# Shifted convolution copies through a DRAM scratch tile, and VectorE operands in the free halves of PSUM banks

## Chip, cores and metric

The kernel runs on one core of a Trainium2 chip, in one launch. The metric is the device time of one execution in microseconds (us). Three executions of the kernel before took 1400.87, 1400.93 and 1402.88 us; the median is 1400.93 us. A core has TensorE (PE in the profile, with its weight loads as PEld), VectorE (DVE), ScalarE (ACT), GpSimd (POOL) and SyncE (SP), which here issues every DMA.

## The reference, cut to what matters

One decoder layer over 256 tokens and 2048 channels in float32. Two head groups read the same projected input; the change touches both.

```python
h = rms_norm(x, norm_mix_pre); z = h @ w_cat
z_rwkv = z + (prev - z) * mu                    # token shift of the first 3360 columns
# RWKV-7 time mixing: 16 heads of 64
kk = heads(k * k_k); kk = kk / max(sqrt(sum(kk*kk)), 1e-12)
y = wkv7_scan(r, decay, k, v, -kk, kk * iclr)   # delta-rule state update, token by token
y = group_norm(y) * gn_gain + gn_bias
y = (y + bonus) * gate
# Conformer convolution: 1024 channels, causal, depthwise, width 31
u = u_lin * sigmoid(u_gate)
c = depthwise_conv(u, dw_w) + dw_b; c = silu(layer_norm(c))
x = x + rms_norm(concat(y, c) @ w_out, norm_mix_post)
# then a squared-ReLU MLP (2048 -> 8192 -> 2048) and a gated embedding of p
```

## The kernel before, in words

**Layout.** Channels lie on the 128 partitions and tokens in the free direction, so a tile is 128 channels by 256 tokens (`T`). Every weight matrix comes in units of 1 MB (16 blocks of 128x128, lines 312 and 384 to 399) into two buffers `W`. `split_stream` (line 401) turns each quarter of a unit into a rounded part `wh` (ACT, line 285) and a remainder `wl` (mostly POOL, line 248), with seven buffers of each. `tile_task` (line 418) multiplies a tile: in the first stage three matmuls of 256 columns for each of 16 blocks (lines 434 to 436), later two matmuls of 512 and 256 columns (lines 439 to 442).

**Order.** The instruction order of each engine is written by a small planner, `Plan` (line 98). Work is given as generators that take buffers (`Take`), wait for conditions (`Wait`) and yield operations with an estimated cost; `run` issues the operation that can start first by the estimates, and among those near it the one of the smallest priority number. The order so found is fixed in each engine's queue. DMAs all go in one queue, SP, in the planner's order (lines 210 to 213): an issue moves the planner's SP clock by 60 ns, and the landing is put 1,900 ns behind the transfer.

**First stage** (to about 555 us). `ORDER` (line 62) lists the input tiles: three for each of eight pairs of heads (`p`), two for each of eight blocks of convolution channels (`c`). All share two PSUM banks `acc`.
- `zshift` (line 619) evicts an input tile of a pair: DVE scales it into `zp` (SBUF, and the bank is free again), ACT makes `zt` = (1-mu) zp, and DVE adds mu times the shifted `zp` (line 252).
- `keys`, `chunk_mats`, `values`, `bonus`, `inverse` and `recur` (lines 692 to 971) do the time mixing of a pair. `recur` runs one pair after the other (`seqlock`) and accumulates in the bank `psy`; ACT copies `psy` to `ysb`, and `group_norm` (line 976) goes on from there, on DVE for most of it.
- `ev_lin` and `ev_gate` (lines 1011, 1021) make `u` = linear part times sigmoid of the gate. `taps` (line 1035) does the convolution as matmuls over four channels-by-shift copies: for each group of 32 channels, four matmuls with columns of the identity matrix put `u`, shifted by 0 to 3 tokens, onto four blocks of 32 partitions in a bank `wk` (line 1044), ACT copies the bank into `cvst` (line 1047, recorded as line 285), and 32 matmuls take the 31 taps from it (line 1056).
- `layer_norm` (line 1066) runs over all eight blocks when the last is done.
- The output projection follows, the convolution half first (`OUT_ORDER`, line 64). Its split input uses the buffer `hl` that the input tiles read, so it waits for the last of them.

**Second stage.** Normalisation, MLP, gate; nothing of it is changed.

Of the kernel before, what the change touches and what calls it, by code (L numbers as in the profile page):

```python
# [16 lines left out]
P = 128  # L17
T = 256
# [79 lines left out]
class Plan:  # L98
# [100 lines left out]
    def issue(self, task, best):  # L199
# [123 lines left out]
def decoder_block(ctx: ExitStack, tc: tile.TileContext, x, p, w_in, w_gd, w_out, w_up, w_down,  # L323
# [225 lines left out]
    pl.static("cv", cvst)  # L549
    def v4(t):  # L550
        return t.rearrange("p (c t) -> p c t", c=NC)
# [62 lines left out]
    def scaled(acc, o, W, cols=P):  # L614
        yield Wait(lambda: "rstd" in S)
        r = S["rstd"]
        yield pl.tt(["DVE"], o, acc.t[:cols, :T], r.t[:cols], ALU.mult, T, [acc, r], [W], [acc])

    def zshift(acc, o, W, mu, j=0, cols=P):
        zp = yield Take("zp", 1)  # L620
        yield pl.memset(zp.t[:, 0:1], 0.0, [(zp, 0)], 1)
        yield from scaled(acc, zp.t[:cols, 1:], zp, cols)
        mu, om = vec(mu, j, rows=cols), omu[:cols, VOFF[mu] + j if VOFF[mu] < 24 else 24 + VOFF[mu] - VOFF["mu_wa"] + j:][:, 0:1]
        d = yield Take("zt", 1)
        yield pl.act(d.t[:cols], zp.t[:cols, 1:], AF.Identity, T, [zp, "omu"], [d], scale=om)
        a, b = zp.t[:cols, 0:T], d.t[:cols]
# [65 lines left out]
    def keys(j):  # L692
# [12 lines left out]
        n4 = yield Take("n4")  # L705
        yield pl.ts(["DVE"], n4.t, psn.t[:, 0:4], 1e-24, None, ALU.max, None, 4, [psn], [n4], [psn])
# [3 lines left out]
        yield pl.act(n4.t, n4.t, AF.Sqrt, 4, [n4], [n4])  # L710
        yield pl.tt(PD, kp.t, kp.t, zk.t, ALU.mult, T, [kp, zk], [kp], [zk])
        rn = yield Take("rn")
        yield pl.vec(80, lambda: nc.vector.reciprocal(n4.t, n4.t), [n4], [n4])
        yield pl.vec(202, lambda: nc.vector.tensor_copy(rn.t, n4.t[:, :, None].to_broadcast([P, 4, C])),
                     [n4], [rn], [n4])
# [79 lines left out]
    def bonus(j):  # L795
# [4 lines left out]
        yield pl.stt(rk.t, zr.t, vec("r_k", j), kp.t, ALU.mult, ALU.mult, T, [zr, kp], [rk], [zr, kp])  # L800
        pb = yield Take("wk")
        yield pl.pe(430, lambda: nc.tensor.matmul(pb.t[:, :T], bones, rk.t, start=True, stop=True),
                    [rk], [pb], [rk])
        bv = yield Take("bv")
# [21 lines left out]
    def inverse(j):  # L826
# [10 lines left out]
        ud = yield Take("ud")  # L837
        yield pl.vec(335, lambda: nc.vector.tensor_reduce(out=ud.t, in_=um.t.rearrange("p c q j -> p c j q"),
                                                          axis=mybir.AxisListType.X, op=ALU.add), [um], [ud], [um])
        udh = yield Take("udh")  # L840
        udl = yield Take("udl")
        yield pl.copy(["DVE"], udh.t, ud.t, 32, [ud], [udh])
        yield pl.tt(["DVE"], udl.t, ud.t, udh.t.bitcast(F32), ALU.subtract, 32, [ud, udh], [udl], [ud])
# [6 lines left out]
        pe = yield Take("inv")  # L850
# [62 lines left out]
    def recur(j):  # L913
# [62 lines left out]
    def group_norm(j, ysb):  # L976
        pr = prs[j]
        X3 = mybir.AxisListType.X
        s4 = yield Take("s4")
        yield pl.vec(335, lambda: nc.vector.tensor_reduce(out=s4.t, in_=ysb.t, axis=X3, op=ALU.add), [ysb], [s4])  # L980
        yield pl.ts(["DVE"], s4.t, s4.t, 1.0 / 64, None, ALU.mult, None, 4, [s4], [s4])
        cen = yield Take("cen")
        yield pl.tt(["DVE"], cen.t, ysb.t, s4.t[:, :, None].to_broadcast([P, 4, C]), ALU.subtract, T,
                    [ysb, s4], [cen], [s4])
# [8 lines left out]
        pgn = yield Take("psy")  # L993
# [27 lines left out]
    def ev_gate(j):  # L1021
        def f(acc):
            gt = yield Take("gt")
            yield from scaled(acc, gt.t, gt)
            yield pl.act(gt.t, gt.t, AF.Sigmoid, T, [gt], [gt])
# [3 lines left out]
            yield pl.tt(PD, lin, lin, gt.t, ALU.mult, T, [gt, u], [u], [gt])  # L1029
# [5 lines left out]
    def taps(j):  # L1035
# [478 lines left out]
```

## Time and profile before

| | |
|---|---|
| median of three runs | 1400.93 us |
| profiled execution, its own time | 1402.03 us |
| its span | 1400.2 us |
| PE busy | 1351.5 us (97%) |
| POOL busy | 1174.2 us (84%) |
| ACT busy | 799.4 us (57%) |
| DVE busy | 736.4 us (53%) |
| DMA moved | 229.40 MB, 164 GB/s |

The profile is that of one execution. Busy time is the union of an engine's instructions. A PE instruction's recorded end is modelled and overlaps its successor, so what an instruction costs PE is read from its start to the next one's start. An idle stretch stands in front of an instruction with what ended it ("<-").

### The profile page before, as it was taken

To read this page: it belongs to the slowest core of one execution; us is meant where nothing else is said; L and a number is where in the kernel's file an instruction comes from. 1 tells how busy PE (TensorE), PEld (TensorE's weight loads), DVE (VectorE), ACT (ScalarE), POOL (GpSimd) and SP (SyncE) were. 2 spreads that over 40 slices of the span, in tenths; PEclk is the share of its full clock that TensorE was granted. 3 is DMA by queue.
4 is the path that set the end of the run, shared out by engine and by line. 5 is a ranking of instruction groups with operands and counts; after the bars stand their busy time and mean duration, and the time that the engine had idled before them with its cause. 6 is when DMAs were issued, how large, how long until landed. Compare 5 with 4: busy or idle time off the path is not lost.

```text
span 1400.2 us, 27458 instructions
## 1 busy us (share of the span) xinstructions
PE 1351.5 (97%) x10476; PEld 1182.8 (84%) x10476; DVE 736.4 (53%) x1305; ACT 799.4 (57%) x1667; POOL 1174.2 (84%) x1002
## 2 busy tenths in 40 slices
PE   8999999999789999999999999999999999999898
PEld 7868878788778998788888888888888888889688
DVE  7256837235886545687003663236632266433694
ACT  6835665556657656855445554455554455555853
POOL 7765756576777769789999999999999999999787
PEclk9999999999899999999999999999999999999999
DMA  7442333433222465345555554555554555555353
GB/s 243 159 140 95 115 130 113 137 110 137 91 99 95 153 248 182 128 160 194 211 182 191 194 185 181 183 189 194 187 181 182 187 194 189 181 181 190 124 198 120
DMA packets 40354, 229.40 MB, mean 164 GB/s; under 512 B 6304, under 2 KB 9632, under 8 KB 14624
## 3 DMA queue, kind: packets, MB, share of 16 engines
q1 hardware_dynamic: 40224, 227.66, 46.0%
q8 instruction: 82, 1.34, 0.4%
q14 instruction: 48, 0.39, 0.1%
HBM read 225.55 MB, written 2.10 MB: 163 GB/s over the span
## 4 chain that ended last, share of the span: by engine, by line
PE 86%; DVE 8%; ACT 2%; issue 1%; DMA 1%; POOL 1%; SPq 0%; DVEq 0%; ACTq 0%; POOLq 0%
PE acc L441 34%; PE acc L442 17%; PE acc L434 8%; PE acc L435 7%; PE acc L436 7%; PE acc L440 3%; PE inv L1056 2%; PE acc L439 1%; PE wk L1044 1%; DVE hl L252 1%; DVE acc L246 1%; DVE acc L252 1%; PE psy L930 1%; PE seq L938 1%; PE wk L749 1%
## 5 line engine op out<-in xcount | busy, mean ns | idle before, releaser
L248 POOL TENSOR_TENSOR wl<-W,wh 128x512 fp32r<-128x512 f32 x548 | 734.4, 1353 | 119.2 <-ACT wh L285 99.3
L285 ACT CAST wh<-W 128x512 fp32r<-128x512 f32 x568 | 346.3, 618 | 220.3 <-PE acc L440 69.0
L441 PE MATMUL acc<-hl,wh 128*128 128x512 f32 x1016 | 369.8, 403 | 11.3 <-DVE hl L252 5.7
L441 PE MATMUL acc<-fhl,wh 128*128 128x512 f32 x806 | 288.2, 395 | 0.0
L442 PE MATMUL acc<-hl,wl 128*128 128x256 f32 x1016 | 286.5, 282 | 0.0
L434 PE MATMUL acc<-hl,wh 128*128 128x256 f32 (+1 forms) x928 | 282.1, 304 | 1.0 <-DVE zp L246 0.9
L436 PE MATMUL acc<-hl,wl 128*128 128x256 f32 (+1 forms) x928 | 265.2, 286 | 6.3 <-POOL wl L248 6.0
L435 PE MATMUL acc<-hl,wh 128*128 128x256 f32 (+1 forms) x928 | 265.7, 286 | 3.2 <-DVE hl L252 2.0
L248 POOL TENSOR_TENSOR wl<-Wb,wh 128x512 fp32r<-128x512 f32 x173 | 237.0, 1380 | 18.4 <-ACT wh L285 11.2
L441 PEld LDWEIGHTS acc<-hl,wh 128*128 128x128 f32 x1016 | 192.1, 189 | 60.2 <-DVE hl L252 8.4
L442 PE MATMUL acc<-fhl,wl 128*128 128x256 f32 x806 | 227.2, 282 | 0.0
L442 PEld LDWEIGHTS acc<-hl,wl 128*128 128x128 f32 x1016 | 193.2, 190 | 3.7
L434 PEld LDWEIGHTS acc<-hl,wh 128*128 128x128 f32 (+1 forms) x928 | 179.2, 193 | 15.6 <-issue 10.1
L246 DVE TENSOR_TENSOR gt<-acc,tb 128x256 f32<-128x256 f32 x124 | 52.4, 423 | 263.7 <-ACT tb L276 263.1
L436 PEld LDWEIGHTS acc<-hl,wl 128*128 128x128 f32 (+1 forms) x928 | 179.1, 193 | 7.3 <-POOL wl L248 6.6
L435 PEld LDWEIGHTS acc<-hl,wh 128*128 128x128 f32 (+1 forms) x928 | 179.5, 193 | 5.4 <-DVE hl L252 3.7
L441 PEld LDWEIGHTS acc<-fhl,wh 128*128 128x128 f32 x806 | 151.5, 188 | 33.4
L285 ACT CAST wh<-Wb 128x512 fp32r<-128x512 f32 x174 | 107.6, 621 | 89.4 <-PE acc L440 35.5
L442 PEld LDWEIGHTS acc<-fhl,wl 128*128 128x128 f32 x806 | 151.3, 188 | 2.7
L246 DVE TENSOR_TENSOR f<-f 128x256 f32<-128x256 f32 x63 | 85.9, 1366 | 1.9
L246 DVE TENSOR_TENSOR fhl<-f,fhl 128x256 fp32r<-128x256 f32 x62 | 58.5, 946 | 26.0 <-ACT fhl L276 26.0
L248 POOL TENSOR_TENSOR wlb<-W,whb 128x512 fp32r<-128x512 f32 x50 | 69.2, 1384 | 1.9 <-ACT whb L285 1.6
(319 smaller groups left out, 2004.2 us busy)
## 6 DMA issues: line engine op xcount, KB each, us to landing
W<-in_w_up_dram SPq DMA_DIRECT2D x43, 1024.0 KB, 4.8
W<-in_w_down_dram SPq DMA_DIRECT2D x42, 1024.0 KB, 4.8
W<-in_w_in_dram SPq DMA_DIRECT2D x38, 1024.0 KB, 4.9
Wb<-in_w_down_dram SPq DMA_DIRECT2D x22, 1024.0 KB, 4.8
Wb<-in_w_up_dram SPq DMA_DIRECT2D x21, 1024.0 KB, 4.8
W<-in_w_out_dram SPq DMA_DIRECT2D x14, 1024.0 KB, 4.8
W<-in_w_gate_dram SPq DMA_DIRECT2D x11, 1024.0 KB, 5.0
Wb<-in_w_gate_dram SPq DMA_DIRECT2D x5, 1024.0 KB, 4.8
```

What stands on the lines that cost most here:

```text
L246: alts.append((e, dve, lambda: nc.vector.tensor_tensor(out=out, in0=a, in1=b, op=op), None, pen))
L248: alts.append((e, 220 + 2.27 * n, lambda: nc.gpsimd.tensor_tensor(out=out, in0=a, in1=b, op=op), None, pen))
L252: return Op([("DVE", 210 + 1.042 * n + (0 if self.from_psum(R) or n < 128 else PORT), lambda: self.nc.vector.scalar_tensor_tensor(out=out, ...
L285: alts.append((e, 150 + 0.835 * n, lambda: self.nc.scalar.copy(out, a), None, 0))
L434: return [nc.tensor.matmul(o, h, xk[:, 0, :], start=(i == 0), stop=False), nc.tensor.matmul(o, h, xk[:, 1, :], start=False, stop=False), n ...
L435: nc.tensor.matmul(o, h, xk[:, 1, :], start=False, stop=False),
L436: nc.tensor.matmul(o, l, xk[:, 0, :], start=False, stop=(i == n - 1))]
L439: return [nc.tensor.matmul(a[:cols, T:], l, xk[:, 0, :], start=False, stop=False), nc.tensor.matmul(a[:cols, :], h, both, start=False, sto ...
L440: nc.tensor.matmul(a[:cols, :], h, both, start=False, stop=True)]
L441: return [nc.tensor.matmul(a[:cols, :], h, both, start=(i == 0), stop=False), nc.tensor.matmul(a[:cols, T:], l, xk[:, 0, :], start=False, ...
L442: nc.tensor.matmul(a[:cols, T:], l, xk[:, 0, :], start=False, stop=False)]
L1056: nc.tensor.matmul(ps.t[32 * g:32 * g + 32, :T], cw.t[:, g, m, :], cv.t[:, g, 4 * m:4 * m + T], start=(m == 0), stop=(m == 7)) for g in ra ...
```

## The change

The four groups of identity matmuls and the two ACT copies of `taps` go. In their place `u` is written to a DRAM tile `ur` (two buffers), and four DMAs read it back, each shifted by one token more, into one block of 32 partitions of `cvst`. These are issued on SP by a new helper `dma_move`, which carries its own estimates; every other DMA now moves the planner's SP clock by 330 ns in place of 60.

Apart from that, operands and results of several DVE steps move to unused columns of PSUM banks that are already held, so that one of two tensor operands lies in PSUM: `zt` (now the second half of the tile's `acc`), the norms `n4` (in the bank `psn`), the sigmoid of the convolution gate (second half of `acc`; its product is now on DVE alone), the diagonal blocks `ud` (in the bank `pe` of `inverse`, taken earlier), the group norm's input (`psy` itself, no `ysb` copy in front) and its last two steps (a bank `wk`, in place of `psy`). The banks are held for longer by as much.

```diff
@@ class Plan: issue
         if eng == "DMA":
-            self.clock["SP"] = st + 60
-            self.dma = max(self.dma, st + 700) + c
-            en = self.dma + 1900
+            self.clock["SP"] = st + (func or 330)
+            if func:
+                en = max(self.dma, st + 700) + c + 3300
+            else:
+                self.dma = max(self.dma, st + 700) + c
+                en = self.dma + 1900
@@ new helper
+    def dma_move(self, dst, src, nbytes, R, W, rel=()):
+        return Op([("DMA", nbytes / 150.0, lambda: self.nc.sync.dma_start(dst, src), 600, 0)], R, W, rel)
@@ decoder_block: pools
+    dr = pa.enter_context(tc.tile_pool(name="dr", bufs=2, space=bass.MemoryType.DRAM))
+    reg(dr, "ur", 2, [P, 3 + T])
@@ zshift (scaled no longer releases acc here: keep=True)
-        yield from scaled(acc, zp.t[:cols, 1:], zp, cols)
+        yield from scaled(acc, zp.t[:cols, 1:], zp, cols, True)
...
-        d = yield Take("zt", 1)
-        yield pl.act(d.t[:cols], zp.t[:cols, 1:], AF.Identity, T, [zp, "omu"], [d], scale=om)
+        d = acc.t[:cols, T:]
+        yield pl.act(d, zp.t[:cols, 1:], AF.Identity, T, [zp, "omu"], [(acc, "d")], scale=om)
...
-        yield pl.stt(o, a, mu, b, ALU.mult, ALU.add, T, [d, zp, (zp, 0), "vt"], [W], [d, zp])
+        yield pl.stt(o, a, mu, b, ALU.mult, ALU.add, T, [(acc, "d"), zp, (zp, 0), "vt"], [W], [acc, zp])
@@ keys
-        n4 = yield Take("n4")
-        yield pl.ts(["DVE"], n4.t, psn.t[:, 0:4], 1e-24, None, ALU.max, None, 4, [psn], [n4], [psn])
+        n4, kn = psn.t[:, 4:8], (psn, "n")
+        yield pl.ts(["DVE"], n4, psn.t[:, 0:4], 1e-24, None, ALU.max, None, 4, [psn], [kn])
...
+        yield pl.vec(202, lambda: nc.vector.tensor_copy(rn.t, n4[:, :, None].to_broadcast([P, 4, C])),
+                     [kn], [rn], [psn])
@@ inverse
-        ud = yield Take("ud")
+        pe = yield Take("inv")
+        ud, kd = pe.t[:, T:T + 32].rearrange("p (c j) -> p c j", c=NC), (pe, "t")
...
-        pe = yield Take("inv")
@@ recur, group_norm
-        ysb = yield Take("ysb")
-        yield pl.copy(["ACT"], ysb.t.rearrange("p a t -> p (a t)"), psy.t[:, :T], T, [(psy, False), (psy, True)], [ysb], [psy])
-        pl.spawn(group_norm(j, ysb), 1.1)
+        pl.spawn(group_norm(j, psy), 1.1)
...
-        pgn = yield Take("psy")
+        pgn = yield Take("wk", 2)
...
-        yield pl.stt(bv.t, pgn.t[:, :T], vec("gn_gain", j), bv.t, ALU.mult, ALU.add, T, [pgn, bv], [bv], [pgn])
+        yield pl.stt(pgn.t[:, T:], pgn.t[:, :T], vec("gn_gain", j), bv.t, ALU.mult, ALU.add, T, [pgn, bv], [(pgn, 1)], [bv, pgn])
...
-        yield pl.stt(y.t[:, j, :], bv.t, vec("gn_bias", j), gs.t, ALU.add, ALU.mult, T, [bv, gs], [(y, j)], [bv, gs])
+        yield pl.stt(y.t[:, j, :], pgn.t[:, T:], vec("gn_bias", j), gs.t, ALU.add, ALU.mult, T, [(pgn, 1), gs], [(y, j)], [pgn, gs])
@@ ev_gate
-            yield from scaled(acc, gt.t, gt)
-            yield pl.act(gt.t, gt.t, AF.Sigmoid, T, [gt], [gt])
+            yield from scaled(acc, gt.t, gt, keep=True)
+            yield pl.act(acc.t[:, T:], gt.t, AF.Sigmoid, T, [gt], [(acc, "d")], [gt])
...
-            yield pl.tt(PD, lin, lin, gt.t, ALU.mult, T, [gt, u], [u], [gt])
+            yield pl.tt(["DVE"], lin, lin, acc.t[:, T:], ALU.mult, T, [(acc, "d"), u], [u], [acc])
@@ taps
-        for b in range(2):
-            pr = yield Take("wk")
-            for g in (2 * b, 2 * b + 1):
-                o = (g % 2) * T
-                yield pl.pe(600, lambda: [
-                    nc.tensor.matmul(pr.t[32 * i:32 * i + 32, o:o + T], ident[:, 32 * g:32 * g + 32],
-                                     u.t[:, i:i + T], start=True, stop=True) for i in range(4)],
-                            [u, (u, 0), "fc"], [pr], [u] if g == 3 else [])
-            yield pl.copy(["ACT"], cv.t[:, 2 * b:2 * b + 2, 28:], pr.t.rearrange("p (g t) -> p g t", g=2), 2 * T,
-                          [pr], [(cv, b)], [pr])
+        ur = yield Take("ur")
+        yield pl.dma_move(ur.t, u.t, P * (3 + T) * 4, [u, (u, 0)], [ur], [u])
+        for i in range(4):
+            yield pl.dma_move(cv.t[32 * i:32 * i + 32, :, 28:], ur.t[:, i:i + T].rearrange("(g c) t -> c g t", g=4),
+                              P * T * 4, [ur], [(cv, i)] + [cv] * (i == 0), [ur] if i == 3 else [])
```

In `inverse` the estimate of the reduction into `ud` goes from 335 to 555 ns, in `keys` that of the reciprocal from 80 to 100. In `bonus` the buffer `bv` is taken before the bank `pb`.

## Rows read from the trace of the kernel before

**Rows 1.** The page's first part: busy time, share of the span and instructions of each engine.
```profile
PE 1351.5 (97%) x10476; PEld 1182.8 (84%) x10476; DVE 736.4 (53%) x1305; ACT 799.4 (57%) x1667; POOL 1174.2 (84%) x1002
```
**Rows 2.** Busy time of each engine in stretches of the span (start and end, length, then busy us and instructions of PE, PEld, DVE, ACT, POOL, the granted clock, the DMA engines' mean share, GB/s).
```profile
42.00:350.00 308.00, 297.55 (x3550) 253.46 (x3550) 164.29 (x387) 181.18 (x388) 201.05 (x220) 0.99 0.37 126
350.00:435.00 85.00, 68.64 (x711) 62.91 (x710) 74.00 (x160) 52.67 (x123) 66.62 (x79) 0.92 0.30 103
435.00:508.00 73.00, 72.97 (x890) 68.99 (x890) 35.78 (x104) 47.37 (x117) 52.79 (x48) 0.98 0.34 121
...
700.00:800.00 100.00, 100.00 (x569) 87.03 (x568) 33.45 (x41) 51.59 (x97) 95.69 (x72) 1.00 0.53 190
```
**Rows 3.** What PE waited for between 350 and 435 us (us in total, times, longest).
```profile
PE acc L436 <- POOL wl L248: 6.0, 3, 4.1
...
PE wk L783 <- ACT vd L276: 1.9, 1, 1.9
```
**Rows 4.** PE in order of time around three of the 23 blocks of copy matmuls (start, length, engine, line, operation, out<-in, count).
```profile
73.83 0.64 PE L1044 MATMUL wk<-u,fc 128*32 128x256 f32 x8
74.40 0.70 PE L802 MATMUL wk<-rk,fc 128*128 128x256 f32 x2
...
78.80 1.52 PE L1044 MATMUL wk<-u,fc 128*32 128x256 f32 x16 [1.87 <-DVE bv L246]
80.25 0.58 PE L434 MATMUL acc<-hl,wh 128*128 128x256 f32 x1
...
97.28 1.07 PE L1044 MATMUL wk<-u,fc 128*32 128x256 f32 x16
98.28 0.39 PE L434 MATMUL acc<-hl,wh 128*128 128x256 f32 x1
98.50 0.28 PE L435 MATMUL acc<-hl,wh 128*128 128x256 f32 x1
98.62 0.28 PE L436 MATMUL acc<-hl,wl 128*128 128x256 f32 x1
```
**Rows 5.** The groups of the copy matmuls and of their weight loads, by line, engine and operation (busy us, mean ns of one | idle before).
```profile
L1044 PE MATMUL wk<-u,fc 128*32 128x256 f32 x256 | 19.1, 395 | 1.9 <-DVE bv L246 1.9
L1044 PEld LDWEIGHTS wk<-u,fc 128*32 128x32 f32 x256 | 6.0, 109 | 6.0 <-DVE bv L246 2.1 <-issue 0.3
```
**Rows 6.** DMA issues (count, KB each, median us from issue to landing).
```profile
W<-in_w_in_dram SPq DMA_DIRECT2D x38, 1024.0 KB, 4.9
out_dram<-os SPq DMA_DIRECT2D x16, 128.0 KB, 1.8
gup<-in_w_gup_dram SPq DMA_DIRECT2D x8, 128.0 KB, 5.1
```
**Rows 7.** What SP's queue waited for, whole span, the largest entry.
```profile
SPq L231 <- POOL wl L248: 1079.9, 184, 19.1
```
**Rows 8.** What ACT waited for between 42 and 350 us: its only wait for a DMA.
```profile
ACT wh L285 <- DMA W<-in_w_in_dram: 0.2, 1, 0.2
```
**Rows 9.** The instructions on some tiles, from the views of one tile each (line, engine, operation, out<-in and count: ns min/median/max, first and last start).
```profile
L252 DVE SCALAR_TENSOR_TENSOR zr<-zp,vt,zt x8: 471/484/1542, 42.5 to 422.0; 128x256 f32<-128x256 f32 x8
L252 DVE SCALAR_TENSOR_TENSOR bv<-psy,vt,bv x8: 474/484/485, 144.2 to 507.1; 128x256 f32<-128x256 f32 x8
L283 DVE CAST udh<-ud x8: 146/544/1306, 88.1 to 463.8; 128x32 fp32r<-128x32 f32 x8
L285 ACT COPY ysb<-psy x8: 356/373/375, 135.1 to 501.3; 128x256 f32<-128x256 f32 x8
L231 SPq DMA_DIRECT2D cw<-in_w_cv_dram x8: 327/355/426, 56.3 to 319.7; - x8
L276 ACT CAST hl<-y x16: 389/401/407, 427.9 to 509.4; 128x256 fp32r<-128x256 f32 x16
L246 DVE TENSOR_TENSOR y<-y,sqt x4: 406/984/1558, 370.3 to 377.7; 128x256 f32<-128x256 f32 x4
```
**Rows 10.** DVE's groups between 350 and 435 us, those that the change touches.
```profile
L252 DVE SCALAR_TENSOR_TENSOR zr<-zp,vt,zt 128x256 f32<-128x256 f32 x3 | 2.4, 804 | 0.7 <-ACT zt L277 0.6
L252 DVE SCALAR_TENSOR_TENSOR vd<-zp,vt,zt 128x256 f32<-128x256 f32 x3 | 2.4, 791 | 0.1
L252 DVE SCALAR_TENSOR_TENSOR zk<-zp,vt,zt 128x256 f32<-128x256 f32 x2 | 2.2, 1110 | 0.0
L283 DVE CAST udh<-ud 128x32 fp32r<-128x32 f32 x2 | 1.5, 744 | 0.0
```
**Rows 11.** DVE and PE in order of time at the end of the first four input tiles.
```profile
38.49 0.76 DVE L246 TENSOR_TENSOR zp<-acc,rstd 128x256 f32<-128x256 f32 x2 [2.06 <-ACT rstd L276]
40.47 0.49 DVE L252 SCALAR_TENSOR_TENSOR wa<-zp,vt,zt 128x256 f32<-128x256 f32 x1 [1.23 <-ACT zt L277]
...
38.97 0.39 PE L434 MATMUL acc<-hl,wh 128*128 128x256 f32 x1 [0.92 <-DVE zp L246]
```
**Rows 12.** DVE in order of time, the longest stretch between the two steps of one `zshift`.
```profile
367.80 0.40 DVE L246 TENSOR_TENSOR zp<-acc,rstd 128x256 f32<-128x256 f32 x1
...
379.91 0.47 DVE L252 SCALAR_TENSOR_TENSOR vd<-zp,vt,zt 128x256 f32<-128x256 f32 x1
```
**Rows 13.** The last step of the last group norm on DVE, and the PE instruction that waited at its end, in order of time.
```profile
507.64 1.10 DVE L252 SCALAR_TENSOR_TENSOR y<-bv,vt,gs 128x256 f32<-128x256 f32 x1
...
511.16 0.39 PE L435 MATMUL acc<-hl,wh 128*128 128x256 f32 x1 [0.94 <-DVE hl L246]
```

More of the change, by code (lines that the diff above doesn't have):

```diff
@@ L612, in x_norm, with scaled @@
         yield pl.act(warm, bias_cache[1e-6], AF.Sigmoid, 1, (), ["warm"])
-    def scaled(acc, o, W, cols=P):
+    def scaled(acc, o, W, cols=P, keep=False):
         yield Wait(lambda: "rstd" in S)
         r = S["rstd"]
-        yield pl.tt(["DVE"], o, acc.t[:cols, :T], r.t[:cols], ALU.mult, T, [acc, r], [W], [acc])
+        yield pl.tt(["DVE"], o, acc.t[:cols, :T], r.t[:cols], ALU.mult, T, [acc, r], [W], [] if keep else [acc])
     def zshift(acc, o, W, mu, j=0, cols=P):
@@ L709, in keys @@
                     [(sg, 1, j), "omka"], [kp])
-        yield pl.act(n4.t, n4.t, AF.Sqrt, 4, [n4], [n4])
+        yield pl.act(n4, n4, AF.Sqrt, 4, [kn], [kn])
         yield pl.tt(PD, kp.t, kp.t, zk.t, ALU.mult, T, [kp, zk], [kp], [zk])
         rn = yield Take("rn")
-        yield pl.vec(80, lambda: nc.vector.reciprocal(n4.t, n4.t), [n4], [n4])
-        yield pl.vec(202, lambda: nc.vector.tensor_copy(rn.t, n4.t[:, :, None].to_broadcast([P, 4, C])),
-                     [n4], [rn], [n4])
+        yield pl.vec(100, lambda: nc.vector.reciprocal(n4, n4), [kn], [kn])
+        yield pl.vec(202, lambda: nc.vector.tensor_copy(rn.t, n4[:, :, None].to_broadcast([P, 4, C])),
+                     [kn], [rn], [psn])
         prn = yield Take("wk")
@@ L800, in bonus @@
         yield pl.stt(rk.t, zr.t, vec("r_k", j), kp.t, ALU.mult, ALU.mult, T, [zr, kp], [rk], [zr, kp])
+        bv = yield Take("bv")
         pb = yield Take("wk")
@@ L803, in bonus @@
                     [rk], [pb], [rk])
-        bv = yield Take("bv")
         yield pl.tt(["DVE"], ck(bv.t), vd.t[:, :, 0, :], ck(pb.t[:, :T]), ALU.mult, T, [pb, vd], [bv], [pb, vd])
@@ L836, in inverse @@
                     m8[:, None, :, None].to_broadcast(sh), ALU.mult, T, Uk + ["fc"], [um])
-        ud = yield Take("ud")
-        yield pl.vec(335, lambda: nc.vector.tensor_reduce(out=ud.t, in_=um.t.rearrange("p c q j -> p c j q"),
-                                                          axis=mybir.AxisListType.X, op=ALU.add), [um], [ud], [um])
+        pe = yield Take("inv")
+        ud, kd = pe.t[:, T:T + 32].rearrange("p (c j) -> p c j", c=NC), (pe, "t")
+        yield pl.vec(555, lambda: nc.vector.tensor_reduce(out=ud, in_=um.t.rearrange("p c q j -> p c j q"),
+                                                          axis=mybir.AxisListType.X, op=ALU.add), [um], [kd], [um])
         udh = yield Take("udh")
         udl = yield Take("udl")
-        yield pl.copy(["DVE"], udh.t, ud.t, 32, [ud], [udh])
-        yield pl.tt(["DVE"], udl.t, ud.t, udh.t.bitcast(F32), ALU.subtract, 32, [ud, udh], [udl], [ud])
+        yield pl.copy(["DVE"], udh.t, ud, 32, [kd], [udh])
+        yield pl.tt(["DVE"], udl.t, ud, udh.t.bitcast(F32), ALU.subtract, 32, [kd, udh], [udl])
         es = []
@@ L971, in recur, with group_norm @@
         seqlock[0] += 1
-        ysb = yield Take("ysb")
-        yield pl.copy(["ACT"], ysb.t.rearrange("p a t -> p (a t)"), psy.t[:, :T], T, [(psy, False), (psy, True)], [ysb], [psy])
-        pl.spawn(group_norm(j, ysb), 1.1)
-    def group_norm(j, ysb):
+        pl.spawn(group_norm(j, psy), 1.1)
+    def group_norm(j, psy):
         pr = prs[j]
+        yv, ky = psy.t[:, :T].rearrange("p (a t) -> p a t", a=4), [(psy, False), (psy, True)]
         X3 = mybir.AxisListType.X
         s4 = yield Take("s4")
-        yield pl.vec(335, lambda: nc.vector.tensor_reduce(out=s4.t, in_=ysb.t, axis=X3, op=ALU.add), [ysb], [s4])
+        yield pl.vec(335, lambda: nc.vector.tensor_reduce(out=s4.t, in_=yv, axis=X3, op=ALU.add), ky, [s4])
         yield pl.ts(["DVE"], s4.t, s4.t, 1.0 / 64, None, ALU.mult, None, 4, [s4], [s4])
         cen = yield Take("cen")
-        yield pl.tt(["DVE"], cen.t, ysb.t, s4.t[:, :, None].to_broadcast([P, 4, C]), ALU.subtract, T,
-                    [ysb, s4], [cen], [s4])
+        yield pl.tt(["DVE"], cen.t, yv, s4.t[:, :, None].to_broadcast([P, 4, C]), ALU.subtract, T,
+                    ky + [s4], [cen], [s4, psy])
+        ysb = yield Take("ysb")
         yield pl.act(ysb.t, cen.t, AF.Square, T, [cen], [ysb])
@@ L1057, in taps @@
                                  start=(m == 0), stop=(m == 7)) for g in range(4)],
-                        [cw, (cv, 0), (cv, 1)], [ps], [cw, cv] if m == 7 else [])
+                        [cw] + [(cv, i) for i in range(4)], [ps], [cw, cv] if m == 7 else [])
         yield pl.act(a, ps.t[:, :T], AF.Identity, T, [ps], [ka], [ps], bias=vec("dw_b", j))
```

8 lines of the change are left out of this document (4 added, 4 removed).

## The prediction

> **What bounds the kernel now.** I read the page's busy times first: PE is busy for 97% of the span, POOL for 84%, ACT and DVE for little over half [rows 1]. An average hides stages, so next came the busy times of stretches [rows 2]. They show four cases. From 42 to 350 us, where all eight convolutions lie, PE is busy for 297.6 of 308 us and DVE for 164: TensorE sets the pace and the others run under it. From 350 to 435 us PE is idle for 85 - 68.6 = 16.4 us, while DVE is busy for 74.0 of 85 us: the steps of VectorE and, behind it, POOL are what PE waits for. The waits of that stretch agree [rows 3]: 6.0 us on POOL's weight remainders are the largest, one of 1.9 us stands in front of a `wk` bank's user. From 435 to 508 us PE is full again, and in the second stage it is 100% busy, which the change doesn't touch. So PE time taken out before 350 us should shorten the whole, and DVE time taken out counts between 350 and 435 us, hardly elsewhere.
>
> **The change part by part.** The sum is made against the profiled execution's 1402.03 us; the median of the runs is 1.1 us lower, which I take off at the end.
>
> *Copies on PE, removed.* What a block of copy matmuls costs is read from its start to the start of what follows [rows 4]: 74.40 - 73.83 = 0.57 us for a block of 8, 98.28 - 97.28 = 1.00 us for one of 16. There are 14 blocks of 8 and 9 of 16, and one of the 16s, behind an idle stretch, took 80.25 - 78.80 = 1.45 us. So 14 x 0.57 + 8 x 1.00 + 1.45 = 17.4 us. (14 x 8 + 9 x 16 = 256, the group's count; its busy time, 19.1 us [rows 5], counts overlapping ends.) All lies where PE is full, and the input tiles behind move up: **-17.4 us**. It is a full gain only if the weights come fast enough for PE to run on; in this stretch ACT's casts waited 0.2 us for a weight DMA, once [rows 8], so the supply has room.
>
> The Trainium skill has a rule that speaks against counting it so. The Trainium skill (Perfetto Trace Analysis, Identifying the Most-Contended Engine) holds that matmul busy time is a poor measure of TensorE's headroom and that the busy share of weight loads is a better one. By it PE would be at 253.5 of 308 us, 82%, in the stretch, and the copies would be worth their loads' 6.0 us; this becomes a rival below.
>
> *Copies on ACT, removed.* Two for each convolution, on an engine busy for 181 of 308 us [rows 2]: nothing on the path.
>
> *DMAs, added.* Eight stores of 132.6 KB and 32 reads of 131.1 KB, 5.3 MB in all, where the DMA engines are busy for 37% [rows 2]. Each of the 40 issues takes SP 0.33 to 0.43 us [rows 9]; SP spends 1,080 us of the span waiting for `W` buffers [rows 7], so issuing costs nothing. Latency: the nearest rows are the 128 KB stores of the output, 1.8 us, and the 128 KB reads of `gup`, 5.1 us [rows 6]. From `u` to the taps it is then 1.8 + 1.8 = 3.6 us at least and 5.1 + 5.1 + 4 x 0.4 = 11.8 us at most; the planner books (132.6 KB at 150 bytes per ns + 0.7 + 3.3) = 4.9 us for each leg, 11.6 us with the four issues, so the taps are placed late enough, and input tiles fill PE meanwhile. For the last convolution no tile hides it in the same way, and the layer norm starts later by these 4 to 12 us; but the layer norm's last product now starts at 377.7 us and the split of its result into `hl`, which the last input tile has to give back, at 427.9 [rows 9], 50 us later. I take nothing.
>
> *The queue.* The four reads wait on SP for the store, and the next weight unit is queued behind them: SP stands still for 1.8 to 5.1 us and issues for 2 us. PE has up to seven split quarters in hand, each 4 x 3 matmuls at 0.12 us from start to start [rows 4], together 10 us. A unit takes 4.9 us to land [rows 6]. So one convolution's stop of 4 to 7 us is covered; if the cover is gone, it costs what exceeds 10 us. I take nothing, with the price under the rivals.
>
> *DVE operands in PSUM.* The same step on 128x256 takes 471 to 1,542 ns with both tensors in SBUF (`zr`), and 474 to 485 ns with one of them in PSUM (`bv`); the cast of `ud`, 32 columns, takes 146 to 1,306 ns [rows 9]. So the moved steps should come to the lower end. Where DVE is the limit, 350 to 435 us, that is 2.4 + 2.4 + 2.2 - 8 x 0.48 = 3.1 us on `zr`, `vd` and `zk`, 1.5 - 2 x 0.18 = 1.1 us on the casts: 4.2 us [rows 10]. Not every one stands in front of PE; the bounds are 0 and all of the 16.4 us of idle time, if the order that the planner finds is a luckier one. I take three quarters of the 4.2: **-3.2 us**. In the other stretches DVE has room, and I count nothing. The gate's product adds at most eight such steps to DVE in place of POOL, there too.
>
> *Banks held longer.* An `acc` is free after the last step of `zshift` instead of the first. There are two; the other takes a tile of 16 x 3 x 0.12 = 5.8 us meanwhile, so a hold beyond that stalls PE. Once it must: the fifth tile started at 38.97 us, just behind the first `zp` step, and `wa`, the step that will free the bank, ended at 40.47 + 0.49 = 40.96 us [rows 11]: **+2.1 us**. Of the other holds the longest now would be 379.91 + 0.47 - 367.80 = 12.6 us [rows 12], 6.8 us too long. Between 0 and 6.8 us I take 0, as that one lies where DVE is to be relieved. `psn` keeps a `wk` bank through a square root, a reciprocal and a copy, eight times, but 16 holds of `wk` by the copies go; `inv` and `psy` are held longer by two or three DVE steps. At most each of the eight stalls PE as long as the one wait in front of a `wk` user did, 1.9 us [rows 3], 15 us; I take nothing, as 16 holds less stand against eight longer ones.
>
> *The last group norm.* It ends the wait of PE at 511 us, 0.94 us long [rows 13]. The ACT copy in front of it (0.37 us [rows 9]) and the slow form of its last step (1.10 against 0.48 us) go, 1.0 us together, so the wait goes: **-0.9 us**. Next there is PE itself.
>
> Sum: -17.4 - 3.2 + 2.1 - 0.9 = -19.4 us, that is 1382.6 us against the profiled execution and **1381.5 us** against the median.
>
> **The rivals.**
> - *The banks eat part of it.* For: two `acc` and two `wk` banks serve everything, and 27 evictions and eight gates hold on longer. Against: the long hold [rows 12] is the longest, and the usual steps of it are 0.5 us each. With the 6.8 us and a quarter of the 15 us above: 1381.5 + 10.6 = 1392, in 1390 to 1398.
> - *Only the loads count.* PE's true limit is its weight loads, and the copies ran in room that stays empty: 6.0 us [rows 5] in place of 17.4, so 1381.5 + 11.4 = 1393. Against: instructions follow the blocks without a gap [rows 4]. The Trainium skill's page named above would have it so.
> - *More than the sum.* In the busy stretch DVE's steps take up to three times their least time [rows 9] and delay POOL's; with 4.2 us less of DVE the waits of PE there and the low clock (0.92 [rows 2]) fall together. If 13 of the 16.4 us go in place of 3.2: about 1371, in 1362 to 1376.
> - *Nothing comes of it.* The freed PE time goes idle, as the chains of the pairs (keys, inverse, recurrence) set the pace: 1400. Against: PE has 10 us idle in the 308 us.
> - *Slower.* SP is in order: a store placed ahead of a weight unit waits for the gate's product on DVE, the reads for the store, and the unit is late. It decides from the point where such a stop is longer than the 10 us of split quarters: with a store that waits 6 us for `u`, 5.1 us to land, 2 us of issues and 4.9 us for the unit, 18 us, it is 8 us too long, and eight of these make 64 us. If half of them fall so: 1381 + 32 = 1413. Against: ACT hardly waits for a DMA now [rows 8], and the planner places a unit first where it can go first.
>
> **How the numbers follow.** Forecast, 1376 to 1390: 0.58. Banks 0.14; loads only 0.03; more 0.12; nothing 0.04; slower 0.09. The range 1367 to 1397 takes in the forecast, the banks, the loads and two thirds of the better case: 0.83. A difference of 0.2% (2.8 us) is about what can be told from none here. Faster by more: 0.58 + 0.14 + 0.03 + 0.12 = 0.87; within: 0.04; slower: 0.09.
>
> **What would show it.** Right: no rows of line 1044, PE in the stretch from 42 us to the last tap still 96% busy or more, and its end some 17 us earlier; casts still waiting for PE and not for `W`; `zr`, `vd`, `zk` and the last step of the group norm all at 0.48 us; idle time of PE at 38 us up to some 3 us; the idle time of the DVE-bound stretch at 12 to 14 us. Wrong: PE waiting for `cvst` or a weight cast waiting for a DMA (the queue); PE waiting for `zk`, `zr`, `vd` in front of line 434 (the banks); the end of the taps 17 us earlier but the end of the first stage not (the chains). A second stage that is longer by more than 1 us would be something that I haven't seen.

## The result and the profile after

The changed kernel took 1370.18 us (median of four runs, 1369.31 to 1371.38) against 1401.91 us for the kernel before on the same chip (now four executions): ratio 0.9772, interval 0.9755 to 0.9789. That is 31.7 us, inside the range of the prediction (1367 to 1397), but below its forecast of 1376 to 1390 and 12 us more than its sum of 19.4. The study is about these 12 us.

The profiled execution took 1369.31 us with a span of 1367.1. Busy times of the whole span, to be held against [rows 1]:

```profile
PE 1327.1 (97%) x10220; PEld 1175.0 (86%) x10220; DVE 716.4 (52%) x1305; ACT 783.2 (57%) x1637; POOL 1170.5 (86%) x1006
```

PE has exactly 256 matmuls less, the copies. The stages, from the tile views (the start of the last tap, of the last `zp` step, of the second stage's first matmul, and the span):

| us | last tap | last input tile | second stage | span |
|---|---|---|---|---|
| before | 342.0 | 429.9 | 559.2 | 1400.2 |
| after | 328.1 | 402.7 | 529.1 | 1367.1 |

So 13.9 us had been gained at the last tap, 27.2 at the last tile, 30.1 at the end of the first stage, and the second stage, which the change doesn't touch, took 838.0 us in place of 841.0. The whole first stage in one line, by the view of stretches (columns as in [rows 2]), of the kernel before:

```profile
0.00:559.20 559.20, 523.22 (x5755) 463.89 (x5755) 330.39 (x741) 340.25 (x752) 393.78 (x419) 0.98 0.41 141
```

and after:

```profile
0.00:529.10 529.10, 503.00 (x5499) 457.36 (x5499) 310.49 (x741) 324.90 (x722) 390.66 (x423) 0.98 0.47 158
```

PE's busy time fell by 523.22 - 503.00 = 20.2 us, its idle time from 559.2 - 523.2 = 36.0 to 26.1, by 9.9. With 3.0 of the second stage that makes the 33.1 us by which the spans differ. The sum had 17.4 for the first, 2.0 for the second and nothing for the third. Stretches of after that answer to [rows 2], moved with the stages:

```profile
42.00:326.00 284.00, 280.60 (x3298) 248.96 (x3297) 152.26 (x390) 171.30 (x365) 200.94 (x221) 0.99 0.49 157
326.00:411.00 85.00, 73.41 (x766) 67.04 (x766) 70.47 (x165) 52.71 (x129) 69.02 (x86) 0.92 0.28 99
411.00:485.00 74.00, 73.96 (x904) 70.61 (x901) 37.56 (x104) 45.95 (x111) 51.76 (x46) 1.00 0.45 168
700.00:800.00 100.00, 100.00 (x572) 87.37 (x571) 52.16 (x59) 53.62 (x103) 97.78 (x73) 1.00 0.52 187
```

Before the last tap PE is now idle for 3.4 us of 284, against 10.4 of 308; in the DVE-bound stretch for 11.6 of 85 in place of 16.4. The last line shows 572 matmuls in 100 us where there were 569.

### The profile page after: what moved, and what is told of

Its sections match the earlier page's. It is cut to its first block, busy times and chain, and to the rows that moved or that the text cites. A ratio compares the mean times of both kernels' runs of the same rounds, so it can differ in the third digit from the quotient of the medians.

```text
span 1367.1 us, 27015 instructions
## 1 busy us (share of the span) xinstructions
PE 1327.1 (97%) x10220; PEld 1175.0 (86%) x10220; DVE 716.4 (52%) x1305; ACT 783.2 (57%) x1637; POOL 1170.5 (86%) x1006
## 4 chain that ended last, share of the span: by engine, by line
PE 86%; DVE 6%; ACT 2%; DMA 2%; POOL 1%; issue 1%; SPq 1%; DVEq 0%; POOLq 0%; ACTq 0%
PE acc L447 35%; PE acc L448 18%; PE acc L440 8%; PE acc L441 7%; PE acc L442 7%; PE acc L446 3%; PE inv L1059 2%; PE acc L445 1%; DMA cvst<-ur 1%; DVE hl L258 1%; DVE acc L252 1%; DVE acc L258 1%; PE seq L946 1%; PE wk L757 1%; DMA mac<-in_x_dram 1%
## 5 line engine op out<-in xcount | busy, mean ns | idle before, releaser
L447 PE MATMUL acc<-hl,wh 128*128 128x512 f32 x1045 | 374.7, 399 | 11.9 <-DVE hl L258 6.7
L447 PE MATMUL acc<-fhl,wh 128*128 128x512 f32 x837 | 297.2, 395 | 0.0
L448 PE MATMUL acc<-hl,wl 128*128 128x256 f32 x1045 | 293.6, 281 | 0.0
L254 POOL TENSOR_TENSOR wl<-Wb,wh 128x512 fp32r<-128x512 f32 x175 | 240.3, 1389 | 13.3 <-ACT wh L291 8.3
L447 PEld LDWEIGHTS acc<-hl,wh 128*128 128x128 f32 x1045 | 196.8, 188 | 60.5 <-DVE hl L258 9.4
L448 PE MATMUL acc<-fhl,wl 128*128 128x256 f32 x837 | 235.5, 281 | 0.0
L448 PEld LDWEIGHTS acc<-hl,wl 128*128 128x128 f32 x1045 | 198.0, 189 | 3.1
L447 PEld LDWEIGHTS acc<-fhl,wh 128*128 128x128 f32 x837 | 157.3, 188 | 34.6
L448 PEld LDWEIGHTS acc<-fhl,wl 128*128 128x128 f32 x837 | 157.1, 188 | 2.9
L254 POOL TENSOR_TENSOR wlb<-W,whb 128x512 fp32r<-128x512 f32 x50 | 65.5, 1310 | 5.8 <-ACT whb L291 5.7
```

Source lines behind the costliest of these rows:

```text
L254: alts.append((e, 220 + 2.27 * n, lambda: nc.gpsimd.tensor_tensor(out=out, in0=a, in1=b, op=op), None, pen))
L447: return [nc.tensor.matmul(a[:cols, :], h, both, start=(i == 0), stop=False), nc.tensor.matmul(a[:cols, T:], l, xk[:, 0, :], start=False, ...
L448: nc.tensor.matmul(a[:cols, T:], l, xk[:, 0, :], start=False, stop=False)]
```

## The experiments

**The parts alone.** First the two halves were run by themselves. Copies through DRAM (with the planner's estimates for them), the rest as before:

```diff
-                    nc.tensor.matmul(pr.t[32 * i:32 * i + 32, o:o + T], ident[:, 32 * g:32 * g + 32],
...
+        yield pl.dma_move(ur.t, u.t, P * (3 + T) * 4, [u, (u, 0)], [ur], [u])
```

> The kernel before with the convolution copies through the DRAM tile and the new DMA estimates; all VectorE operands stay where they were. Theory (the two parts add up; the copies are worth the 17.4 us of their blocks and some 0.2 us of switching for each of the 23 blocks, 21 us in all): some 1380 us, 1376 to 1384, with the taps' end 15 us earlier than before and the stretch behind it as long as before. Rival (the two parts only pay together, since the stretch behind the taps waits for VectorE): 1390 us or more. Second stage: 841 us from its first matmul to the end, as before, if the shorter 838 us of the changed kernel come from where its SBUF tiles lie.

Measured: 1393.06 us, ratio 0.9934 (0.992 to 0.9949). The gain of 9.6 us is little more than half of what the copies were to bring, and the time lies in the rival's range. And the PSUM operands alone, the changed kernel with the old copies and estimates:

```diff
-        yield pl.dma_move(ur.t, u.t, P * (3 + T) * 4, [u, (u, 0)], [ur], [u])
...
+                    nc.tensor.matmul(pr.t[32 * i:32 * i + 32, o:o + T], ident[:, 32 * g:32 * g + 32],
```

> The changed kernel with the identity matmuls and the ACT copies back in taps and the old DMA estimates; all PSUM operands stay. Theory (additive): 1402 less some 8 us of idle time and 3 us of the second stage, 1391 us, 1387 to 1396. Rival (VectorE's steps only matter once PE has room): 1399 to 1402. Rival (the longer holds of acc and wk cost as long as the copies use wk too): above 1402. Second stage 838 us if the layout of SBUF sets it.

Measured: 1394.73 us, 0.9949 (0.9934 to 0.9965), 7.9 us. Its second stage took 840.9 us, so the 3.0 us of the second stage don't come from where the tiles lie in SBUF. The two gains add up to 17.5 us, and 14 us seemed to belong to neither part.

**The price of the copies.** Each block of copy matmuls of the kernel before issued twice:

```diff
+                    nc.tensor.matmul(pr.t[32 * i:32 * i + 32, o:o + T], ident[:, 32 * g:32 * g + 32],
+                                     u.t[:, i:i + T], start=True, stop=True) for i in range(4)] + [
                     nc.tensor.matmul(pr.t[32 * i:32 * i + 32, o:o + T], ident[:, 32 * g:32 * g + 32],
```

> The kernel before with each block of copy matmuls issued twice in a row (same result). It prices the copies where they stand: theory (PE sets the pace): 14 blocks of 8 get 0.43 us longer and 9 of 16 get 0.86 us, 13.8 us, so 1414 to 1418 us. Rival (only the weight loads count): 6 us, 1408. Rival (the copies run in room that PE has anyway): 1402.

Measured: 1418.94 us, 1.0118 (1.0099 to 1.0137), or 16.3 us more, just above the theory's range. In the first stage PE's busy time rose from 523.22 to 538.40, by 15.2 us. But the 16.3 us aren't the price of the copies alone. From the start of each block to the start of what follows, the blocks take 31.2 us in place of 17.4, so 13.8 more, as expected; the last tap comes 12.5 us later (354.5 against 342.0), the last input tile only 5.6 (435.5 against 429.9), and 11.8 us more are lost between that tile and the second stage, where this kernel has a delay that is told below (the hold of a bank). So the copies cost TensorE what their blocks take from start to start, and not their loads' 6.0; the total can't be read as their price.

**The SP estimate.** The kernel before with SP's clock moved by 330 ns a DMA in the planner:

```diff
-            self.clock["SP"] = st + 60
+            self.clock["SP"] = st + 330
```

> The kernel before with one number of the planner changed: every DMA moves its SP clock by 330 ns in place of 60. Theory: the order hardly matters, 1400 to 1404 us. Rival (what was gained beyond the forecast is a luckier order): the time moves by 4 us or more for this alone.

Measured: 1401.99 us, 0.9999 (0.9989 to 1.0008). The order of every engine came out the same as before, so this run says that the estimate does nothing, and not, as I had read it at first, that the order doesn't matter.

**Parts added and taken away.** The waits in the copies alone pointed at the group norm, so single parts of the PSUM change were added to the copies or taken from the whole: the group norm with `bonus` (its hunk below), and `zshift`.

```diff
-        pgn = yield Take("psy")
+        pgn = yield Take("wk", 2)
...
+        bv = yield Take("bv")
         pb = yield Take("wk")
...
-        bv = yield Take("bv")
```

> The copies through DRAM, and of the PSUM part only the group norm (it reads psy itself, no ysb copy in front, its transposes go to a wk bank, its last two steps read PSUM). The two parts alone gave 9.6 and 7.9 us, both together 31.7, so 14 us belong to neither alone. Theory 'group norm': in the run with the copies alone PE waited 3.8 us in front of the group norm's transposes, and the time from the last input tile to the end of the last recurrence was 84.5 us instead of 71.2; the bank psy, held through a copy and taken a second time by the transposes, keeps the recurrences of the last pairs back once the input tiles end sooner. It expects that stretch at 62 to 72 us and 1379 to 1384 us in all. Rival 'evictions': the DVE steps of zshift are what counts; this run stays at 1388 to 1394. Rival 'spread': each part gives a few us and none is the key; 1386 to 1390.

Measured: 1371.09 us, 0.9775 (0.9759 to 0.9791): the whole effect.

> The changed kernel with the group norm as before (ysb copy, transposes in psy, SBUF operands). Theory 'group norm': the 14 us are lost again, 1380 to 1387 us, with the stretch from the last input tile to the last recurrence at 75 us or more instead of 62.1. Rivals 'evictions' and 'spread': 1371 to 1377 us.

Measured: 1369.51 us, 0.9762 (0.9747 to 0.9776): the whole effect too. The group norm suffices and isn't needed. For `zshift` the edit is:

```diff
-        d = yield Take("zt", 1)
-        yield pl.act(d.t[:cols], zp.t[:cols, 1:], AF.Identity, T, [zp, "omu"], [d], scale=om)
+        d = acc.t[:cols, T:]
+        yield pl.act(d, zp.t[:cols, 1:], AF.Identity, T, [zp, "omu"], [(acc, "d")], scale=om)
```

> The copies through DRAM, and of the PSUM part only zshift (zt in the second half of acc, the bank held until its last step). Theory 'group norm': 1388 to 1394 us, that is no better than the copies alone (1393.1), with 2 us lost at the fifth tile. Rival 'evictions': 1379 to 1384, with the idle time of PE between the last taps and the last input tile down from 12.8 us. Rival 'spread': 1386 to 1390.

Measured: 1382.72 us, 0.9856 (0.984 to 0.9872).

> The changed kernel with zshift as before (zt in SBUF, acc free after its first step). Theory 'group norm': 1368 to 1374 us, and the wait of PE in front of the fifth tile down from 2.9 to about 0.9 us. Rival 'evictions': 1380 to 1387 us, zr, vd and zk again at up to 1.5 us a step. Rival 'spread': 1373 to 1378.

Measured: 1373.73 us, 0.9792 (0.9777 to 0.9806). All three theories have misses here. Every kernel with something added to the copies is quicker than the copies alone, whatever it is. That suggested that not the parts but the order of the copies alone was at fault.

**The same operations in other orders.** One number of the planner was changed. That leaves the operations as they are, but for up to some twenty small steps that the planner gives to another engine, and moves their order on every engine:

```diff
-                en = max(self.dma, st + 700) + c + 3300
+                en = max(self.dma, st + 700) + c + 2300
```

> The copies alone, as in the run that gave 1393.1, with one number of the planner changed (the landing of a move, 3,300 to 2,300 ns): the same operations in another order on every engine. Adding the group norm alone to the copies took 22 us off, zshift alone 10, everything but the group norm 24, everything but zshift 20; so hardly a part is needed for the 14 us. Theory 'order': the copies alone had got an unlucky order, other orders of the same operations lie between 1370 and 1388 us, and the 14 us are no property of the PSUM operands. Rival 'operands': without PSUM operands the chains are too slow in any order: 1390 to 1396.

Measured: 1395.52 us, 0.9954 (0.9939 to 0.9969), as slow as the first order, and in the range of the rival 'operands'. With 4300 in that place:

> The copies alone again, with the landing of a move put at 4,300 ns: a third order. Theory 'order': 1370 to 1388 us, and not the time of the second order to 0.3%. Rival 'operands': 1390 to 1396.

Measured: 1372.20 us, 0.9782 (0.9767 to 0.9796): the copies alone, with none of the moved operands in PSUM, give the time of the whole change (0.9755 to 0.9789). And the kernel before with `self.dma + 2900` in place of 1900:

> The kernel before with the landing of every DMA put 1,000 ns later in the planner: the same operations in another order. (The run with the clock of SP at 330 ns had turned out to leave the order as it was.) Theory 'order': the time moves by more than 3 us, to anywhere from 1385 to 1410, since the order decides some 10 us of idle time. Rival 'operands': 1399 to 1405, as waits behind long DVE steps come in any order.

Measured: 1394.14 us, 0.9936 (0.992 to 0.9953). The kernel before wins 8.6 us, as much as the PSUM operands alone had seemed to bring, with nothing changed but its order.

**What the slow orders have in common.** In order of time (start, length, engine, line, operation, out<-in), the copies alone at 1393 us, from the last pair's bonus product to its chunk matrices:

```profile
416.96 0.63 PE L810 MATMUL wk<-rk,fc 128*128 128x256 f32 x1
...
447.98 0.29 PE L938 MATMUL psy<-SAV,rbst 128*64 128x64 f32 x4
...
449.01 0.38 PE L1002 MATMUL psy<-fc,cen 128*128 128x128 f32 x2
449.43 0.48 DVE L258 SCALAR_TENSOR_TENSOR bv<-psy,vt,bv 128x256 f32<-128x256 f32 x1 [0.27 <-PE psy L1002]
450.29 1.60 DVE L258 SCALAR_TENSOR_TENSOR y<-bv,vt,gs 128x256 f32<-128x256 f32 x1
...
452.14 0.41 DVE L252 TENSOR_TENSOR bv<-vd,wk 128x256 f32<-128x256 f32 x1
...
452.19 0.48 PE L757 MATMUL wk<-arK,BK 64*128 64x128 f32 x2
```

Read it from the end. `chunk_mats` (line 757) takes both `wk` banks before it issues anything. `bonus` had one of them from 416.96 on, for its product, and only then took `bv`; there are two `bv`, and it got one when the group norm of the pair two before gave its `bv` up, with `y<-bv` at 450.29. That group norm wanted the one bank `psy` for its transposes, and the recurrence of the pair between had `psy` until 447.98. So a bank stood still for 452.14 - 416.96 = 35.2 us, and the last pair's chunk matrices, its inverse and its recurrence came late. The order at 1372 us has the transposes ahead of that recurrence:

```profile
412.35 0.59 PE L810 MATMUL wk<-rk,fc 128*128 128x256 f32 x2
...
424.34 0.38 PE L1002 MATMUL psy<-fc,cen 128*128 128x128 f32 x2
...
426.65 0.40 DVE L252 TENSOR_TENSOR bv<-vd,wk 128x256 f32<-128x256 f32 x1
...
427.01 0.60 PE L757 MATMUL wk<-arK,BK 64*128 64x128 f32 x5
```

The bank is held for 14.3 us and the chunk matrices start 25 us earlier. The second slow order shows the hold again, 39.0 us, and the second half of the matmuls waiting for the step that gives the bank back:

```profile
413.86 0.80 PE L810 MATMUL wk<-rk,fc 128*128 128x256 f32 x1
...
452.86 0.41 DVE L252 TENSOR_TENSOR bv<-vd,wk 128x256 f32<-128x256 f32 x1
...
453.32 0.49 PE L757 MATMUL wk<-arK,BK 64*128 64x128 f32 x4 [1.51 <-DVE bv L252]
```

In the kernel before the hold is 455.50 - 435.83 = 19.7 us:

```profile
435.83 0.63 PE L802 MATMUL wk<-rk,fc 128*128 128x256 f32 x1
...
455.50 0.86 PE L749 MATMUL wk<-arK,BK 64*128 64x128 f32 x4
455.50 0.42 DVE L246 TENSOR_TENSOR bv<-vd,wk 128x256 f32<-128x256 f32 x1
```

And in the changed kernel, where `bonus` takes `bv` first and the group norm has no need of `psy`, 2.6 us, behind the chunk matrices:

```profile
418.00 0.71 PE L757 MATMUL wk<-arK,BK 64*128 64x128 f32 x8
...
423.59 0.67 PE L811 MATMUL wk<-rk,fc 128*128 128x256 f32 x2
...
426.18 0.41 DVE L252 TENSOR_TENSOR bv<-vd,wk 128x256 f32<-128x256 f32 x1
```

The kernels in one table, without the one with the SP estimate, which has the order of the kernel before (last pair: the hold of the bank from the product's start to the `bv` step's start, the first chunk matrix; tail: from the last input tile, its last `zp` step, to the second stage's first matmul; PE busy and idle up to that matmul; the second stage to the end of the span):

| kernel | us | hold | chunk matrices | tail | PE busy | PE idle | second stage |
|---|---|---|---|---|---|---|---|
| before | 1401.9 | 19.7 | 455.5 | 129.3 | 523.2 | 36.0 | 841.0 |
| before, other order | 1394.1 | 17.9 | 445.5 | 127.6 | 520.5 | 29.8 | 838.9 |
| before, copies twice | 1418.9 | 35.4 | 476.8 | 141.1 | 538.4 | 38.2 | 840.8 |
| PSUM alone | 1394.7 | 4.3 | 449.8 | 129.8 | 523.4 | 30.7 | 840.9 |
| copies alone, first order | 1393.1 | 35.2 | 452.2 | 141.0 | 510.5 | 40.3 | 840.8 |
| copies alone, second order | 1395.5 | 39.0 | 451.3 | 143.9 | 512.6 | 40.9 | 841.0 |
| copies alone, third order | 1372.2 | 14.3 | 427.0 | 127.7 | 502.5 | 29.8 | 837.6 |
| copies and zshift | 1382.7 | 11.3 | 432.1 | 124.1 | 504.6 | 35.4 | 839.6 |
| copies, group norm and bonus | 1371.1 | 0.8 | 421.0 | 125.4 | 501.5 | 27.6 | 839.5 |
| after without these two | 1369.5 | 14.5 | 425.1 | 128.4 | 502.0 | 28.3 | 837.7 |
| after without zshift | 1373.7 | 3.3 | 427.6 | 126.5 | 504.5 | 27.6 | 838.0 |
| after | 1370.2 | 2.6 | 418.0 | 126.4 | 503.0 | 26.1 | 838.0 |
| after, early acc (below) | 1368.7 | 2.6 | 414.8 | 126.3 | 499.2 | 26.7 | 838.2 |

The three kernels with a hold of over 30 us are the only three in which, for the last pairs, those transposes come behind the recurrence of the pair between, and they stand apart in the tail: 141 to 144 us, where the ten others take 124 to 130. In the slow orders of the copies alone the last input tile came 20 us earlier than in the kernel before (409.8 and 409.6 against 429.9 us), so the gain of the copies was there and was lost behind it. Of the 18.5 us that the first order lies behind the third at the second stage, 13.3 are tail. The tail, and in it 24 us around the end of the last pair's recurrence (columns as in [rows 2]), in the first order:

```profile
409.80:550.80 141.00, 128.18 (x1324) 120.99 (x1324) 67.73 (x164) 84.83 (x203) 103.68 (x92) 0.94 0.42 155
484.00:508.00 24.00, 16.29 (x117) 14.54 (x116) 9.75 (x24) 9.16 (x25) 8.49 (x8) 0.72 0.38 140
```

and in the third:

```profile
404.60:532.30 127.70, 122.28 (x1321) 117.26 (x1321) 69.83 (x178) 83.75 (x203) 101.55 (x91) 0.98 0.48 177
462.00:486.00 24.00, 24.00 (x222) 23.55 (x221) 9.50 (x23) 14.29 (x34) 17.50 (x14) 1.00 0.56 207
```

In the first order PE has nothing but the late recurrence between 484.4 us and its end at 494.6 (472.5 in the third order): it waits between the steps, and then 3.8 us for the group norm behind it. After the first of these waits the granted clock is 0.5 (1.2 GHz) from 489 to 503 us, and even the matmuls of 256 columns that fill PE again behind the waits start 0.21 us apart in place of 0.12. So the 13.3 us are 7.4 of idle time and 5.9 of busy time, with a granted clock of 0.94 in place of 0.98; the busy times of the table hold the clock as well as the work.

A long hold isn't a price by itself. In the kernel with `zshift` in between PE lost idle time to one a pair earlier, where `bonus` held a bank from 360.71 to 371.78 us. Its waits of PE between 337 and 540 us (us in total, times, longest) begin so:

```profile
PE wk L777 <- DVE bv L252: 6.1, 2, 5.6
```

The third order and the changed kernel without `zshift` hold a bank as long for that pair, 15.7 and 16.0 us, and PE waits no longer than 1.6 us for a `wk` there. Nor did the 19.7 us of the kernel before lengthen its tail. So the hold goes with what the copies alone lost in two of their orders, and doesn't explain what made the kernel before slow: of the 30.1 us that the change had gained at the second stage, 27.2 lie ahead of the last tile. Up to there PE was idle for 30.6 us before and for 21.2 after; in the other order of the kernel before it was 24.8. That idle time is made of many waits of at most some 4 us, and what in the order makes them stays open.

The table is no proof that the hold alone makes the longer tail, as a new order changes more than one thing. The copies alone with only the two lines of `bonus` exchanged would tell it, and weren't run.

**A version with the fifth tile freed.** The first three tiles (`wa` and the two of `gd`) make `zt` in SBUF again:

```diff
-        yield from zshift(acc, wa, "wa", "mu_wa")
+        yield from zshift(acc, wa, "wa", "mu_wa", early=True)
...
+        if early:
+            zt = yield Take("zt", 1)
+            d, kd = zt.t[:cols], zt
```

> The changed kernel, where the first three tiles (wa and the two gd) make zt in SBUF again and give acc back after the first step. My sum: the fifth tile's wait falls from 2.9 to about 0.9 us, and the whole by 2: 1367 to 1369. Theory 'order': the fifth tile's wait falls, but the total moves by up to 5 us to either side, as the order changes with it: 1365 to 1376.

Measured: 1368.73 us, 0.9757 (0.9742 to 0.9771). The wait before the fifth tile fell from 2.9 to 0.9 us. The interval overlaps that of the changed kernel, so the 2 us fit, but aren't shown by the time; and PE's idle time up to the second stage didn't fall with the wait (26.7 us against 26.1), only its busy time did, at a granted clock of 0.99 in place of 0.98.

## Why the prediction was right in sign and short by 12 us

*Copies on PE, -17.4: right, as far as it can be told.* PE's busy time in the first stage fell by 20.2 us in the changed kernel and by 20.8 in the third order of the copies alone, but only by 12.7 and 10.6 in the two slow orders, where the granted clock is 0.97 in place of 0.98. Doubled, the blocks took 13.8 us more from start to start. A part that the term had left out can be read in [rows 4]: the matmul behind a block takes 98.50 - 98.28 = 0.22 us to the next where its like takes 0.12, so such a block costs some 0.1 us more than its own length. The last tap came 13.9 us earlier, not 17, but the last tile behind it 27.2: how far the taps lie ahead of the tiles is the order's choice. The rival "only the loads count" falls: by it, doubling would have cost 6.0 us, and the last tap came 12.5 us later; and in all three orders of the copies alone the last tile came 20 to 25 us earlier (13 to 18 against the other order of the kernel before). The Trainium skill's rule (Perfetto Trace Analysis, Identifying the Most-Contended Engine), as the prediction applied it, would have given that 6.0; here the trace disagrees with it.

*DMAs and queue, 0: right.* The instructions of `ur` and `cvst` in the view of these tiles (count, ns min/median/max, first and last start), and their landing:

```profile
L237 SPq DMA_DIRECT2D cvst<-ur x32: 326/434/739, 82.7 to 314.7; - x32
L237 SPq DMA_DIRECT2D ur<-u x8: 326/327/382, 79.6 to 311.2; - x8
...
DMA to landing us min/median/max: 1.8/5.7/7.7
```

PE waited for `cvst` for 1.2 us in all, as the waits up to 330 us show (us in total, times, longest), together with the fifth tile:

```profile
PE acc L440 <- DVE wa L258: 2.9, 1, 2.9
...
PE inv L1059 <- DMA cvst<-ur: 1.2, 2, 0.6
```

SP stood still for `u` for 33.6 us in seven waits, the longest 7.1, and ACT's casts waited 0.8 us for a weight DMA: covered. So the stops that the rival "slower" named came, and cost next to nothing.

*The fifth tile, +2.1: right.* 2.9 against 0.92 us [rows 11] is 2.0.

*Other holds of acc, 0: wrong by 4.5.* I had set it between 0 and 6.8 us and taken 0. From 328 to 529 us PE waited:

```profile
PE acc L440 <- DVE zr L258: 4.5, 1, 4.5
```

It is the sign that the prediction had named for the banks. Not all of it is the price of the longer hold: in the first order of the copies alone, where the bank comes free after the first step, PE waited 3.9 us for `zp` at 373 us.

*The last group norm, -0.9: right, but its reason isn't shown.* No wait on `hl` is left there; none is left either in the third order of the copies alone, which has the old group norm.

*DVE operands, -3.2: the step that failed.* The steps came out as forecast, all short, `zr` at 466 to 482 ns where [rows 9] has up to 1,542:

```profile
L258 DVE SCALAR_TENSOR_TENSOR zr<-zp,vt,acc x7: 466/479/482, 117.7 to 393.6; 128x256 f32<-128x256 f32 x7
...
L258 DVE SCALAR_TENSOR_TENSOR vd<-zp,vt,acc x7: 468/481/482, 128.2 to 404.7; 128x256 f32<-128x256 f32 x7
...
L258 DVE SCALAR_TENSOR_TENSOR zk<-zp,vt,acc x8: 479/480/482, 41.6 to 383.4; 128x256 f32<-128x256 f32 x8
```

But no gain from them is shown. Up to the second stage the third order of the copies alone has DVE busy for 328.19 us and the changed kernel for 310.49, 17.7 less, and their times are the same within the intervals. The PSUM operands alone were worth what another order of the kernel before was worth. Nor did the idle time fall only where the term had put it: 7.0 us lie before the last tap (10.4 to 3.4), where the prediction had counted nothing, and 4.8 in the DVE-bound stretch. The rival "more than the sum" gave the right time, 1371, for a reason that isn't shown. PE's idle time is 36.0 us in the kernel before, and 29.8 both in its other order and in the third order of the copies alone, all three with both tensors of `zshift`'s last step in SBUF. So 6.2 of the 9.9 us need no shorter step, and whether the 3.7 down to 26.1 are the operands' isn't shown. The prediction had named a "luckier order" as a bound and then priced the term by step times: the order was what counted, and it was put at nothing. That 1370 lies in the range is in part luck, as two of the three orders of the copies alone gave 1393.1 and 1395.5. The prediction's part on banks asked how long each bank would be held by the change, and not who already held one while it waited for something else. The two lines of `bonus` and the move of `pgn` keep that hold short in the changed kernel (2.6 us), but without them it is 14.5 us and the time the same.

*The second stage, 0: wrong by 3.0.* It takes 837.6 to 841.0 us over these kernels, and it goes with PE's own order there. Six kernels, the SP estimate among them, have the same matmuls in the same order in that stage, tile by tile, and took 840.8 to 841.0 us; four others share a second order and took 837.6 to 838.9. From 700 to 1200 us the matmuls of 512 columns follow each other at 234.9 ns in the first order of the copies alone and at 233.1 in the third, from start to start. The largest group of them (busy us, mean ns), in the first:

```profile
L447 PE MATMUL acc<-hl,wh 128*128 128x512 f32 x624 | 223.6, 399 | 0.0
```

and the third:

```profile
L447 PE MATMUL acc<-hl,wh 128*128 128x512 f32 x624 | 221.5, 395 | 0.0
```

What in the order does it stays open.

## What to carry to other kernels

Where a planner writes the order, a change moves the order too, and here the order alone was worth 8.6 us in one kernel and up to 23 in another: run the same operations in two or three orders before a gain is put down to an edit. Look for a task that takes a scarce buffer and then waits for another one; taking the scarce one last keeps it from standing still, though no run here has that edit alone. Work that is taken from a full engine is worth its time from start to start, once nothing behind it is held up.

## What the runs showed of the hardware that I had not expected

Matmuls of one shape, 128x512 on an engine that is busy for 100%, followed each other at 234.9 or 233.1 ns, with the same operations in another order, and that made most of the 3 us of the second stage.
